# The recurrent gates' products one step behind the rounding of their tokens, and a head's squares in a buffer of their own

## The chip, the cores and the metric

The kernel runs on one core of a Trainium2 chip. Its time is the device time of one execution in microseconds (us). Three runs of the kernel before took 1630.3 to 1632.11 us, their median is 1631.26 us. Beside them stands one profiled execution of 1630.65 us.

The engines are named as the profile does: PE is TensorE (the matrix products), PEld its weight loads, DVE is VectorE, ACT is ScalarE, POOL is GpSimd, SP is the engine that issues most DMAs. Each engine takes its instructions in the order in which the program issued them to it; semaphores hold an instruction back until what it reads is there and what it overwrites has been read.

## What is computed

One layer of a diffusion backbone with 256 latent tokens, 256 context tokens and 2048 channels, all in float32. A mixer joins two groups: eight HGRN2 heads (a gated linear recurrence with a 128x128 state in both directions) and eight RG-LRU blocks. A GEGLU network with a convolution follows. What the change touches, cut to its core:

```python
def rglru_dir(xc, wa, ba, wx, bx, lam, h0):          # eight blocks of 128 channels, two directions
    r = sigmoid(einsum(xb, wa) + ba)                 # "the gates": two products per direction
    i = sigmoid(einsum(xb, wx) + bx)
    log_a = -RG_C * r * softplus(-lam)
    bterm = sqrt(-expm1(2.0 * log_a)) * i * xc
    h = linear_scan(exp(log_a), bterm, h0)

def hgrn2_readout(o, g, hg_g):                       # per head of 128 channels
    o = rmsnorm(o, hg_g)                             # needs the sum of o*o over the head's channels
    return o * silu(g)

out = concatenate([hg_l, rg_l]) @ w_out              # x += gate * rmsnorm(out), then the GEGLU network
```

`xc` is a depthwise convolution of width 4 along the tokens. The product of the layer's input with `w_in` gives 56 column blocks of 128 channels: for each head `q`, `zf`, `zb`, `v` and `g`, for each recurrent block `rx` and `rg`.

## The kernel before

Channels lie on the 128 partitions and tokens along the free axis: 256 latent tokens, with 256 context tokens behind them where they are needed. Every float32 product is made of three faster ones: weights and tokens are each split into a rounded part and the rest (`wh`, `wl` and `hh`, `hl`), and a chunk of 128 input channels gives `wh*hh + wh*hl + wl*hh` (lines 266 to 268, three matmuls of 512 or 256 columns).

**The main list.** `entries` lists the weight blocks in the order of use. The mixer's part (some 195 to 760 us) is 50 entries of `w_in`, written out in `ORDER`. A block of 1 MB lands in one of three buffers. ACT rounds each half to `wh` (line 165; for the `rg` blocks DVE does, line 163), and DVE subtracts for `wl` (line 180). Four such halves are kept, and they are split two halves ahead of use.

**Steps.** An entry of 512 tokens has four steps of 12 matmuls, one of 256 tokens two steps of 24. `run()` does three things in each step: it splits weights ahead, it calls `step()`, and it issues the step's main matmuls. `step()` lets each generator in `gens` go on to its next `yield`. So what a generator issues between two yields stands, on every engine, just before the main matmuls of one step. These matmuls are what PE has to do while other engines prepare the generator's next piece. A step of the mixer has about 2.7 us of main matmuls.

**Generators.** Three kinds run side by side in the mixer:

- `rg_all` goes through the eight recurrent blocks, one after another, with `rg_chain`. A block makes its convolution on ACT and DVE, rounds the result to `xh` (line 767) and the rest to `xl` (line 768), and `gates(0)` issues six matmuls of 512 columns (lines 776 to 778) into two banks of PSUM. Then, for each direction: two sigmoids read the banks (line 786), tanh, exp and a sum on ACT (lines 788 to 790), DVE arithmetic and a square root on ACT, and two scans on DVE. The second direction's six matmuls come at the end of the first direction's last step.
- `tree` does one head: a tree of elementwise products with copies on ACT (line 918, `kc` and `qc`) and small matmuls (line 902), then the state products (941) and the output products (951). After these, ACT copies the output and squares it (956), PE sums the squares over the channels with a column of ones (960), and DVE copies the two sums to `ssq` (961). The squares lie in the first half of `qa`, the head's tile of products of query and decay (DVE writes it for the next head in line 872). `hdone` then tells `norms` that the head has its sums.
- `mod2_all` multiplies modulation weights on DVE (line 689, 180 instructions in the whole kernel).

A `g` block's generator applies silu on ACT (975), spreads the head's scale over the partitions with two small matmuls (line 589) into a PSUM bank, and multiplies on DVE (978 and 980).

**Banks.** `sbank()` hands out two banks in turn, `sd0` and `sd1`. In the mixer they serve the gates (both at once) and, in its last part, the spread of the `g` blocks. The tag `qc` has three buffers, taken in turn.

Of the kernel before, what the change touches and what calls it, by code (L numbers as in the profile page):

```python
# [9 lines left out]
F32 = mybir.dt.float32  # L10
F32R = mybir.dt.float32r
U8 = mybir.dt.uint8
AF = mybir.ActivationFunctionType
# [5 lines left out]
T = 256  # L19
# [30 lines left out]
def dit_block_kernel(  # L50
# [20 lines left out]
    pe, act, dve, pool = nc.tensor, nc.scalar, nc.vector, nc.gpsimd  # L71
# [22 lines left out]
    def sbank(which=None):  # L94

        if which is None:
            which = turn["s"] = 1 - turn["s"]
        return pss.tile([128, 512], F32, name="sd", tag=f"sd{which}")
# [7 lines left out]
    def P(name, k=0, n=1):  # L106
        o = _SM[name] + k
        return sm[:, o:o + n]
# [312 lines left out]
    for i, (name, b) in enumerate(ORDER):  # L421
        add_s1(win[i], h1, 512 if name in ("rx", "zf", "zb", "v") else 256,
               lambda ps, name=name, b=b: afters[name](b, ps), hi="dve" if name == "rg" else "act")
# [95 lines left out]
    sp4, sp8 = P("c", 0, 16), P("c", 16, 16)  # L519
# [214 lines left out]
    hq = hp2_cm.__enter__()  # L734
# [4 lines left out]
    def wg_fetch(b):  # L739
        if b < NH:  # L740
            wgs[b] = hq.tile([128, 4, 128], F32, name="wg", tag="wg")
            nc.sync.dma_start(wgs[b], wgate[b])
# [3 lines left out]
    def rg_all():  # L746
        for b in range(NH):
            while b not in rgsrc:
                yield
            yield from rg_chain(b, rgsrc[b].rearrange("p (a t) -> p a t", a=2))  # L750
            ydone.add(b)

    def rg_chain(b, x):
        xh, xl, wh, wl = (hq.tile([128, 512], F32R, name=n, tag=n) for n in ("xh", "xl", "gh", "gl"))
        wg = wgs[b].rearrange("p a n -> p (a n)")
        act.activation(wh, wg, AF.Copy)
        dve.tensor_tensor(wl, wg, wh.bitcast(F32), op=OP.subtract)
        wg_fetch(b + 1)
        xc = hq.tile([128, 2, T], F32, name="xc", tag="xc")
        act.activation(xc, x, AF.Identity, scale=P("cw", 16 + b), bias=P("cb", b))  # L760
        for j, o, i in ((0, slice(2, T), slice(0, T - 2)), (1, slice(1, T), slice(0, T - 1)),
                        (3, slice(0, T - 1), slice(1, T))):
            dve.scalar_tensor_tensor(xc[:, :, o], x[:, :, i], P("cw", 8 * j + b), xc[:, :, o], op0=OP.mult, op1=OP.add)
            if j == 0:
                yield
        xf = xc.rearrange("p a t -> p (a t)")
        dve.tensor_copy(xh, xf)
        dve.tensor_tensor(xl, xf, xh.bitcast(F32), op=OP.subtract)
        yield

        def gates(d):
            pg = {}
            for w in (1, 0):
                pg[w] = sbank()
                c = slice((2 * d + w) * 128, (2 * d + w + 1) * 128)
                pe.matmul(pg[w], wh[:, c], xh, start=True, stop=False)
                pe.matmul(pg[w], wh[:, c], xl, start=False, stop=False)
                pe.matmul(pg[w], wl[:, c], xh, start=False, stop=True)
            return pg
        pg = gates(0)  # L780
        yield
        for d in range(2):
            k = 8 * d + b
            r, iv, th, t = (hq.tile([128, 512], F32, name=n, tag=n) for n in ("r", "iv", "th", "t"))
            for w, dst, bn in ((1, iv, "bx"), (0, r, "ba")):
                act.activation(dst, pg[w], AF.Sigmoid, bias=P(bn, k))
            yield
            act.activation(th, r, AF.Tanh, scale=sp4[:, k:k + 1])
            act.activation(r, r, AF.Exp, scale=sp8[:, k:k + 1])
            act.activation(r, r, AF.Identity, bias=ones)  # L790
            dve.tensor_tensor(iv, iv, xf, op=OP.mult)
            yield

            dve.scalar_tensor_tensor(t, th, 1.0, r, op0=OP.add, op1=OP.mult)
            dve.scalar_tensor_tensor(r, t, 4.0, r, op0=OP.subtract, op1=OP.mult)
            dve.tensor_scalar(t, r, -0.5, -1.0, op0=OP.mult, op1=OP.add)
            yield
            act.activation(th, th, AF.Sqrt)
            dve.tensor_tensor(r, r, iv, op=OP.mult)
            yield  # L800
            dve.scalar_tensor_tensor(th, th, -0.5, r, op0=OP.mult, op1=OP.mult)
            if d == 0:
                dve.tensor_tensor_scan(r[:, T:], t[:, T:], th[:, T:], 0.0, op0=OP.mult, op1=OP.add)
                dve.tensor_tensor_scan(yt[:, b, :], t[:, :T], th[:, :T], r[:, 511:512], op0=OP.mult, op1=OP.add)
            else:
                dve.tensor_tensor_scan(r[:, ::-1], t[:, ::-1], th[:, ::-1], 0.0, op0=OP.mult, op1=OP.add)
            if d == 0:
                pg = gates(1)
            yield
        dve.tensor_tensor(yt[:, b, :], yt[:, b, :], r[:, :T], op=OP.add)  # L810
# [46 lines left out]
    def q_gen(h, ps):  # L857
        while h and h - 1 not in last_product:
            yield
        q = hq.tile([128, T], F32, name="q", tag="q")  # L860
        act.activation(q, ps, AF.Sigmoid)
        yield
        dve.tensor_tensor(q, q, ps, op=OP.mult)
        yield from tree(h, q)

    def tree(h, q):
        f, k, v = hd[h]["f"], hd[h]["k"], hd[h]["v"]
        qa = hq.tile([128, 2, T], F32, name="qa", tag="qa")
# [19 lines left out]
        kc, qc = {}, {}  # L888
# [63 lines left out]
        last_product.add(h)  # L952
        yield
        act.activation(ot[:, h, :], po, AF.Copy)
        sq = qa[:, 0, :]
        act.activation(sq, po, AF.Square)
        yield
        pq = lbank()
        for b in range(2):
            pe.matmul(pq[:, b:b + 1], sq[:, b * 128:(b + 1) * 128], ones, start=True, stop=True)  # L960
        dve.tensor_copy(ssq[:, 2 * h:2 * h + 2], pq[:, 0:2])
        del hd[h]
        hdone.add(h)
# [380 lines left out]
```

## Time and profile before

| what | us |
|---|---|
| median of three runs | 1631.26 |
| profiled execution | 1630.65 |
| its span, first to last instruction | 1628.9 |
| PE busy in the span | 1566.8 |
| PEld busy | 1371.2 |
| DVE busy | 1207.4 |
| ACT busy | 891.8 |

The profiled execution is 1.75 us longer than its span: this lies ahead of the first instruction and behind the last. In a table by stretch, each line gives the stretch, its length, and for PE, PEld, DVE, ACT and POOL the busy time with the number of instructions; `PEclk` is the clock that TensorE was granted, 1.00 being 2.4 GHz and 0.50 being 1.2 GHz. Busy time is a sum over stages with different limits, so the waits of a stretch say more about it than its share. An instruction's idle time before it, in brackets in a timeline, is the time in which its engine did nothing, and the name behind the arrow is what ended it. `L776` is line 776 of the kernel.

### The profile page before, as it was taken

What the parts mean: (1) busy time and instruction counts of PE and PEld (TensorE: products, weight loads), DVE (VectorE), ACT (ScalarE), POOL (GpSimd) and SP (SyncE); (2) the same over time, 40 slices, a digit from 0 to 9 for tenths busy, and PEclk for the clock granted to TensorE, in tenths of its full rate; (3) what the DMA queues carried; (4) which work ended last, traced back from release to release, by engine and by line L of the source; (5) the groups of instructions that cost most, each with busy time, mean ns of one, the idle gap of its engine ahead of it and who ended that gap; (6) DMA issues with size and microseconds to landing.
All of it is one profiled execution on the core that took longest, in us unless ns stands there. A gap on an engine that the chain in (4) does not pass through costs nothing.

```text
span 1628.9 us, 25405 instructions
## 1 busy us (share of the span) xinstructions
PE 1566.8 (96%) x9904; PEld 1371.2 (84%) x9904; DVE 1207.4 (74%) x2033; ACT 891.8 (55%) x1284; POOL 121.0 (7%) x101
## 2 busy tenths in 40 slices
PE   7999899999999999899999999999999999999997
PEld 1355687778788888799999999999999999888886
DVE  2666597889888769678658788888888877656656
ACT  2355685767674456486455644444444445455553
POOL 0511000000000000000220111111111111000000
PEclk9999999999999999999999999999999999999999
DMA  8676544455455565536862466666666555655552
GB/s 355 236 283 225 193 162 149 158 172 174 167 197 199 183 206 186 183 124 238 318 224 94 171 228 230 226 231 226 229 227 227 201 181 190 221 184 197 191 200 110
DMA packets 75584, 329.66 MB, mean 202 GB/s; under 512 B 8392, under 2 KB 8520, under 8 KB 45128
## 3 DMA queue, kind: packets, MB, share of 16 engines
q1 hardware_dynamic: 75176, 327.53, 56.9%
q8 instruction: 77, 1.26, 0.3%
q10 hardware_dynamic: 288, 0.52, 0.1%
q14 instruction: 43, 0.35, 0.1%
HBM read 325.92 MB, written 2.10 MB: 201 GB/s over the span
## 4 chain that ended last, share of the span: by engine, by line
PE 79%; DVE 11%; ACT 4%; issue 3%; DMA 2%; POOL 1%; SPq 0%; DVEq 0%; ACTq 0%; POOLq 0%
PE mb L266 12%; PE mb L267 12%; PE mb L268 12%; PE mb L458 5%; PE lv L266 5%; PE lv L267 5%; PE lv L268 5%; PE lv L458 4%; PE sd L458 4%; PE sd L317 3%; DVE wl L180 2%; PE xb L458 2%; DVE macc L689 2%; PE sd L324 1%; PE sd L323 1%
## 5 line engine op out<-in xcount | busy, mean ns | idle before, releaser
L165 ACT ACTIVATE wh<-wf 128x1024 fp32r<-128x1024 f32 x424 | 445.3, 1058 | 508.4 <-PE mb L267 166.5
L180 DVE TENSOR_TENSOR wl<-wf,wh 128x1024 fp32r<-128x1024 f32 x440 | 535.7, 1223 | 155.1 <-ACT wh L165 151.2
L266 PE MATMUL mb<-hh,wh 128*128 128x512 f32 (+1 forms) x800 | 282.9, 354 | 0.0
L268 PE MATMUL mb<-hh,wl 128*128 128x512 f32 (+1 forms) x800 | 273.4, 342 | 0.0
L267 PE MATMUL mb<-hl,wh 128*128 128x512 f32 (+1 forms) x800 | 273.2, 342 | 0.0
L266 PE MATMUL mb<-h2h,wh 128*128 128x258 f32 x672 | 190.6, 284 | 0.0
L268 PE MATMUL mb<-h2h,wl 128*128 128x258 f32 x672 | 190.2, 283 | 0.0
L267 PE MATMUL mb<-h2l,wh 128*128 128x258 f32 x672 | 190.1, 283 | 0.0
L266 PE MATMUL lv<-h2h,wh 128*128 128x258 f32 x656 | 186.0, 284 | 0.0
L268 PE MATMUL lv<-h2h,wl 128*128 128x258 f32 x656 | 185.6, 283 | 0.0
L267 PE MATMUL lv<-h2l,wh 128*128 128x258 f32 x656 | 185.5, 283 | 0.0
L268 PEld LDWEIGHTS mb<-hh,wl 128*128 128x128 f32 x800 | 152.8, 191 | 17.9
L267 PEld LDWEIGHTS mb<-hl,wh 128*128 128x128 f32 x800 | 153.7, 192 | 15.9
L266 PEld LDWEIGHTS mb<-hh,wh 128*128 128x128 f32 x800 | 153.5, 192 | 15.3
L689 DVE SCALAR_TENSOR_TENSOR macc<-wm,cs,macc 128x512 f32<-128x512 f32 x180 | 136.3, 757 | 7.3 <-DMA wm<-in_wmod_dram 6.2
L267 PEld LDWEIGHTS mb<-h2l,wh 128*128 128x128 f32 x672 | 127.4, 190 | 0.0
L268 PEld LDWEIGHTS mb<-h2h,wl 128*128 128x128 f32 x672 | 126.9, 189 | 0.0
L266 PEld LDWEIGHTS mb<-h2h,wh 128*128 128x128 f32 x672 | 126.8, 189 | 0.0
L267 PEld LDWEIGHTS lv<-h2l,wh 128*128 128x128 f32 x656 | 124.4, 190 | 0.0
L268 PEld LDWEIGHTS lv<-h2h,wl 128*128 128x128 f32 x656 | 123.9, 189 | 0.0
L266 PEld LDWEIGHTS lv<-h2h,wh 128*128 128x128 f32 x656 | 123.7, 189 | 0.0
L1040 DVE TENSOR_TENSOR al<-actt,ah 128x256 fp32r<-128x256 f32 x88 | 37.8, 431 | 86.2 <-ACT ah L1039 86.2
(344 smaller groups left out, 2861.8 us busy)
## 6 DMA issues: line engine op xcount, KB each, us to landing
wf<-in_wup_dram SPq DMA_DIRECT2D x88, 1024.0 KB, 4.9
wm<-in_wmod_dram SPq DMA_DIRECT2D x256, 256.0 KB, 5.1
wf<-in_win_dram SPq DMA_DIRECT2D x50, 1024.0 KB, 4.8
wf<-in_wdn_dram SPq DMA_DIRECT2D x44, 1024.0 KB, 4.8
wf<-in_wmod_dram SPq DMA_DIRECT2D x32, 1024.0 KB, 5.7
wf<-in_wout_dram SPq DMA_DIRECT2D x16, 1024.0 KB, 5.1
wf<-in_wearly_dram SPq DMA_DIRECT2D x12, 512.0 KB, 5.5
oy<-in_xs_dram SPq DMA_DIRECT2D x2, 1024.0 KB, 13.4
```

The costliest lines, as they stand in the source:

```text
L165: act.activation(wh, w, AF.Copy)
L180: lo.tensor_tensor(wl, fetched[j][:, h * H:(h + 1) * H], wh.bitcast(F32), op=OP.subtract)
L266: pe.matmul(ps, wh[:, w], hh, start=(i == 0), stop=False)
L267: pe.matmul(ps, wh[:, w], hl, start=False, stop=False)
L268: pe.matmul(ps, wl[:, w], hh, start=False, stop=(i == KC - 1))
L317: pe.matmul(ps, cs[:, :, 4 * q + k], get[:, k * 512:(k + 1) * 512], start=(q == 0 and k == 0), stop=(q == 3 and k == 3))
L323: pe.matmul(ps, cc, wh[:, s], start=(q == 0 and k == 0), stop=False)
L324: pe.matmul(ps, cc, wl[:, s], start=False, stop=(q == 3 and k == 3))
L458: pe.matmul(dn["ps" + str(half)][tb * 2 + n], a[:, t], w[:, s], start=(kc == 0 and first), stop=(kc == NJ - 1 and last))
L689: dve.scalar_tensor_tensor(acc, w, cc, acc, op0=OP.mult, op1=OP.add)
L1040: dve.tensor_tensor(al, actt[:, kc, :], ah.bitcast(F32), op=OP.subtract)
```

## The change

Four edits, all in generators of the mixer:

- `rg_chain` has a `yield` between the rounding of the tokens and `gates(0)`. The six matmuls are issued in the next step, behind one step's main matmuls, and everything behind them in the block comes one step later. A block has one step more.
- In each direction, the tanh moves ahead of a `yield`, into the step of the two sigmoids.
- The squares of a head go to a buffer of the tag `qc` instead of the first half of `qa`.
- The copy to `ssq` comes a step behind the matmuls whose sums it reads, and `hdone` with it.

```diff
--- before.py
+++ after.py
@@ -777,6 +777,7 @@
                 pe.matmul(pg[w], wh[:, c], xl, start=False, stop=False)
                 pe.matmul(pg[w], wl[:, c], xh, start=False, stop=True)
             return pg
+        yield
         pg = gates(0)
         yield
         for d in range(2):
@@ -784,8 +785,8 @@
             r, iv, th, t = (hq.tile([128, 512], F32, name=n, tag=n) for n in ("r", "iv", "th", "t"))
             for w, dst, bn in ((1, iv, "bx"), (0, r, "ba")):
                 act.activation(dst, pg[w], AF.Sigmoid, bias=P(bn, k))
-            yield
             act.activation(th, r, AF.Tanh, scale=sp4[:, k:k + 1])
+            yield
             act.activation(r, r, AF.Exp, scale=sp8[:, k:k + 1])
             act.activation(r, r, AF.Identity, bias=ones)
             dve.tensor_tensor(iv, iv, xf, op=OP.mult)
@@ -952,12 +953,13 @@
         last_product.add(h)
         yield
         act.activation(ot[:, h, :], po, AF.Copy)
-        sq = qa[:, 0, :]
+        sq = hq.tile([128, T], F32, name="qc", tag="qc", bufs=3)
         act.activation(sq, po, AF.Square)
         yield
         pq = lbank()
         for b in range(2):
             pe.matmul(pq[:, b:b + 1], sq[:, b * 128:(b + 1) * 128], ones, start=True, stop=True)
+        yield
         dve.tensor_copy(ssq[:, 2 * h:2 * h + 2], pq[:, 0:2])
         del hd[h]
         hdone.add(h)
```


Behind the first added line the numbers of the changed kernel are one higher than before, behind the second two: the copy to `ssq` is line 963 there, the matmul with the ones 961, silu 977.

A row below is an instruction: its line, its operation, what it writes and reads by the program's names, its shape, and a count where it repeats.

The first place is PE's queue around the first direction's gates of the last recurrent block, where the spread of the first `g` block stands too. Before, the six matmuls of the gates come directly behind the spread:

```order
L902 MATMUL lv<-qc,kc 128x128 x2
L589 MATMUL sd<-ident,rso 128x128 x2
L776 MATMUL sd<-xh,gh 128x512
L777 MATMUL sd<-xl,gh 128x512
L778 MATMUL sd<-xh,gl 128x512
L776 MATMUL sd<-xh,gh 128x512
L777 MATMUL sd<-xl,gh 128x512
L778 MATMUL sd<-xh,gl 128x512
L266 MATMUL mb<-hh,wh 128x256
```


In the changed kernel main matmuls follow the spread (here of 256 columns, the first three of 24):

```order
L903 MATMUL lv<-qc,kc 128x128 x2
L589 MATMUL sd<-ident,rso 128x128 x2
L266 MATMUL mb<-hh,wh 128x256
L267 MATMUL mb<-hl,wh 128x256
L268 MATMUL mb<-hh,wl 128x256
```


and the gates come behind these 24 and the next level of the head's tree:

```order
L903 MATMUL lv<-qc,kc 128x128 x2
L776 MATMUL sd<-xh,gh 128x512
L777 MATMUL sd<-xl,gh 128x512
L778 MATMUL sd<-xh,gl 128x512
L776 MATMUL sd<-xh,gh 128x512
L777 MATMUL sd<-xl,gh 128x512
L778 MATMUL sd<-xh,gl 128x512
L266 MATMUL mb<-hh,wh 128x256
```


The gates have moved by one step. In the blocks before, where one block follows the other directly, the steps add up against the heads: the first block's gates stand 12 main matmuls of 512 columns later than before, and the second block's first gates have moved from the step ahead of the head's state product (941) to a step behind it.

The second place is DVE's queue around the first head's copy to `ssq`. Before, the block's arithmetic (801 to 804) and the next head's start (863 to 872) stand behind it:

```order
L689 SCALAR_TENSOR_TENSOR macc<-wm,cs,macc 128x512 x2
L180 TENSOR_TENSOR wl<-wf,wh 128x1024
L961 COPY ssq<-lv 128x2
L801 SCALAR_TENSOR_TENSOR th<-th,r 128x512
L803 SCALAR_TENSOR_TENSOR r<-t,th 128x256
L804 SCALAR_TENSOR_TENSOR oy<-t,r,th 128x256
L689 SCALAR_TENSOR_TENSOR macc<-wm,cs,macc 128x512
L711 TENSOR_TENSOR gg_1159<-rq,sm 128x4
L713 TENSOR_TENSOR gg_1159<-gg_1159,sm 128x4
L863 TENSOR_TENSOR q<-q,mb 128x256
L871 TENSOR_TENSOR ks<-k 128x256
L872 TENSOR_TENSOR qa<-f,q 128x512
```


In the changed kernel other work of the block (795 to 797) and the modulation come ahead of it:

```order
L795 SCALAR_TENSOR_TENSOR t<-th,r 128x512
L796 SCALAR_TENSOR_TENSOR r<-t,r 128x512
L797 TENSOR_SCALAR t<-r 128x512
L689 SCALAR_TENSOR_TENSOR macc<-wm,cs,macc 128x512
L711 TENSOR_TENSOR gg_1159<-rq,sm 128x4
L713 TENSOR_TENSOR gg_1159<-gg_1159,sm 128x4
L963 COPY ssq<-lv 128x2
L864 TENSOR_TENSOR q<-q,mb 128x256
L872 TENSOR_TENSOR ks<-k 128x256
L873 TENSOR_TENSOR qa<-f,q 128x512
```


The copy has moved behind a step's DVE work, and the matmul that it waits for stands a step ahead on PE.

The third place is ACT's queue from the first silu on, around the sigmoids (786) of the last block's first direction, which free the two banks `sd0` and `sd1`. Before:

```order
L975 ACT_TABLE_LOAD
L975 ACTIVATE gl<-mb 128x256
L918 ACTIVATE kc<-k 128x256
L918 ACTIVATE qc<-qa 128x256
L786 ACT_TABLE_LOAD
L786 ACTIVATE iv<-sd,sm 128x512
L786 ACTIVATE r<-sd,sm 128x512
L918 ACTIVATE kc<-k 128x256
L918 ACTIVATE qc<-qa 128x256
```


In the changed kernel:

```order
L977 ACT_TABLE_LOAD
L977 ACTIVATE gl<-mb 128x256
L919 ACTIVATE kc<-k 128x256
L919 ACTIVATE qc<-qa 128x256
L919 ACTIVATE kc<-k 128x256
L919 ACTIVATE qc<-qa 128x256
L977 ACTIVATE gl<-mb 128x256
L787 ACT_TABLE_LOAD
L787 ACTIVATE iv<-sd,sm 128x512
L787 ACTIVATE r<-sd,sm 128x512
L788 ACTIVATE th<-r,sm 128x512
```


Ahead of the load of the sigmoids' table there now stand a second pair of the tree's copies (919) and the second silu, and the tanh comes directly behind the sigmoids. Counted over the whole queue, ACT has 83 table loads instead of 82. On PE, in the same place, the spread of the second `g` block stands one step behind the gates instead of two.

## Rows read from the trace of the kernel before

**Rows 1.** The page's first lines: busy time, share of the span, instructions.

```profile
span 1628.9 us, 25405 instructions
PE 1566.8 (96%) x9904; PEld 1371.2 (84%) x9904; DVE 1207.4 (74%) x2033; ACT 891.8 (55%) x1284; POOL 121.0 (7%) x101
```

**Rows 2.** Busy time in four stretches, then granted clock, DMA share, GB/s.

```profile
200.00:300.00 100.00, 94.21 (x457) 78.61 (x456) 83.74 (x147) 69.69 (x103) 0.00 (x0) 0.96 0.47 160
300.00:400.00 100.00, 95.70 (x517) 82.15 (x517) 86.60 (x153) 71.65 (x105) 0.00 (x0) 0.97 0.51 172
600.00:700.00 100.00, 91.63 (x553) 81.09 (x552) 80.96 (x148) 62.01 (x95) 0.00 (x0) 0.95 0.53 180
700.00:745.00 45.00, 45.00 (x376) 44.54 (x376) 36.98 (x61) 33.43 (x43) 0.00 (x0) 1.00 0.39 138
```

**Rows 3.** TensorE's waits from 190 to 745 us: total, times, longest.

```profile
PE sd L776 <- DVE xh L767: 16.7, 6, 4.5
PE sd L776 <- DVE oy L980: 4.1, 1, 4.1
PE lv L902 <- DVE ad L891: 2.0, 2, 1.5
PE lv L941 <- DVE qa L936: 1.8, 1, 1.8
PE xb L704 <- ACT v L850: 1.6, 1, 1.6
```

**Rows 4.** TensorE's timeline at single stalls: start, duration, in brackets idle time.

```profile
199.58 0.76 PE L776 MATMUL sd<-xh,gh 128*128 128x512 f32 x1 [4.46 <-DVE xh L767]
246.49 0.47 PE L776 MATMUL sd<-xh,gh 128*128 128x512 f32 x1 [1.51 <-DVE xh L767]
299.44 0.47 PE L776 MATMUL sd<-xh,gh 128*128 128x512 f32 x1 [1.98 <-DVE xh L767]
349.74 0.47 PE L776 MATMUL sd<-xh,gh 128*128 128x512 f32 x1 [2.09 <-DVE xh L767]
447.93 0.76 PE L776 MATMUL sd<-xh,gh 128*128 128x512 f32 x1 [3.95 <-DVE xh L767]
685.92 0.65 PE L776 MATMUL sd<-xh,gh 128*128 128x512 f32 x1 [2.75 <-DVE xh L767]
691.87 0.79 PE L776 MATMUL sd<-xh,gh 128*128 128x512 f32 x1 [4.09 <-DVE oy L980]
```

**Rows 5.** Stretches behind four stalls, one of full clock; columns as before.

```profile
199.60:204.70 5.10, 5.10 (x12) 3.75 (x13) 5.10 (x9) 3.93 (x7) 0.00 (x0) 0.50 0.84 307
300.40:303.70 3.30, 3.30 (x13) 2.86 (x12) 3.27 (x8) 2.62 (x5) 0.00 (x0) 0.50 0.38 108
448.00:453.90 5.90, 5.90 (x14) 4.36 (x15) 5.86 (x13) 0.72 (x2) 0.00 (x0) 0.50 0.84 307
692.00:696.20 4.20, 4.20 (x17) 3.91 (x18) 2.95 (x8) 2.67 (x5) 0.00 (x0) 0.50 0.08 12
205.00:210.10 5.10, 5.10 (x24) 4.19 (x23) 5.03 (x8) 3.00 (x5) 0.00 (x0) 1.00 0.24 78
```

**Rows 6.** VectorE's waits from 190 to 745 us.

```profile
DVE ssq L961 <- PE lv L960: 16.5, 4, 5.7
DVE qa L872 <- PE lv L960: 11.2, 3, 4.4
```

**Rows 7.** Timelines of VectorE and TensorE near 248 us.

```profile
247.65 0.42 DVE L936 TENSOR_TENSOR qa<-qa,tn 128x256 f32<-128x256 f32 x1
251.13 1.24 PE L941 MATMUL lv<-qa,k 128*128 128x256 f32 x5
```

**Rows 8.** Timelines of ScalarE and TensorE in the last block.

```profile
694.25 1.28 ACT L786 ACT_TABLE_LOAD   x1
695.54 0.69 ACT L786 ACTIVATE iv<-sd,sm 128x512 f32<-128x512 f32 x1
701.20 0.61 PE L589 MATMUL sd<-ident,rso 128*128 128x128 f32 x4
```

More of the change, by code (lines that the diff above doesn't have):

```diff
@@ L786, in rg_chain @@
                 act.activation(dst, pg[w], AF.Sigmoid, bias=P(bn, k))
+            act.activation(th, r, AF.Tanh, scale=sp4[:, k:k + 1])
             yield
-            act.activation(th, r, AF.Tanh, scale=sp4[:, k:k + 1])
             act.activation(r, r, AF.Exp, scale=sp8[:, k:k + 1])
```

## The prediction

> **What bounds the kernel now.** I read the page's busy times first: PE is busy for 1566.8 of 1628.9 us [rows 1], so at most 62 us of idle time can go, and what else can go is time in which its clock is low. The table by stretch comes next, to see where that is [rows 2]. In the mixer's part PE is busy for 94 of 100 us, then 96, and for 92 between 600 and 700 us, at a mean clock of 0.95 to 0.97. From 700 to 745 us it is never idle. The change touches only this part; behind it I count nothing.
>
> The list of PE's waits says what ends its idle time there [rows 3]. The first matmul of the gates (L776) waits six times for the rounding `xh` on DVE, 16.7 us in all, and once for 4.1 us for the multiplication that still reads its bank (L980). All other waits come to 2.0 + 1.8 + 1.6 = 5.4 us. The timeline gives the seven stalls one by one: 4.46, 1.51, 1.98, 2.09, 3.95, 2.75, and 4.09 us [rows 4].
>
> A stall costs more than its idle time. In the 5.1 us behind the first one the clock is 0.50, which is 1.2 GHz, and 12 matmuls go through; from 205 us on, in as long a stretch at full clock, 24 do [rows 5]. Such a stretch therefore loses half its length. Behind the stall at 299.44 there are 3.3 us of it (and as much behind that at 349.74), behind the stall at 447.93 there are 5.9, and behind the last one 4.2. Behind that at 246.49 there is none. In every case PE had been idle just before.
>
> DVE's waits are the other half of the picture [rows 6]. It waits 16.5 us in four places for PE's sum of squares, to copy it, and 11.2 us in three places to overwrite `qa`, which that sum still reads. DVE takes its work in order, so in these 27.7 us it does nothing for PE, and a block's `xh` comes late afterwards.
>
> **The change part by part.** *The gates a step later.* No matmul is added. Between the rounding and the gates there now stand the main matmuls of one step, 12 of 512 columns. At full clock 24 such matmuls lie in 5.1 us [rows 5]; the stretch cuts one or two of them at its edges, so 12 take 2.7 us. What is left of a stall is its length less 2.7, as long as DVE's work ahead of `xh` is as late as before:
>
> - At 199.58: 4.46 - 2.7 leaves 1.8 us, so 2.7 us are gained. Its low clock costs half of 5.1, that is 2.55 us. A shorter idle time can give back all or nothing of it, and I take half, 1.3. Together 4.0 (bounds 2.7 and 5.25).
> - At 246.49: 1.51 goes. What is late next is the head's state product (L941), which now meets PE before the gates do. It starts at 251.13, and its operand is ready at 247.65 + 0.42 = 248.07 [rows 7]. Without the stall, and with the gates' six matmuls (1.4 us) behind it instead of ahead, it would start at 248.2: just in time. Gain 1.5 (bounds 0 and 1.5).
> - At 299.44: 1.98, and half of 3.3 for the clock, 1.65. Gain 3.6 (without the clock 2.0).
> - At 349.74: 2.09 and 1.65. Gain 3.75 (without the clock 2.1).
> - At 447.93: 2.7 from the step. Of the 1.25 that are left I leave half, 0.6, because DVE comes sooner (below). The low clock costs half of 5.9, 2.95. Gain 3.95 - 0.6 + 2.95 = 6.3 (bounds 2.7 and 6.9).
>
> These five come to 4.0 + 1.5 + 3.6 + 3.75 + 6.3 = 19.15 us.
>
> *The last block, 685.92 and 691.87.* Here I expect nothing. The step takes the 2.7 us away from the first stall, but the second matmul of the gates still needs the bank that L980 frees, and PE would reach it no earlier than before. The next spread (L589, at 701.20) needs a bank that the block's first sigmoid frees, at 695.54 + 0.69 = 696.23 [rows 8]: 5.0 us in hand. It will stand one step nearer to the gates, which takes 2.7 of these, and before that sigmoid ACT has to do three more activations (a pair of copies and a silu of 256 columns, each at most the 0.69 us of the sigmoid with 512: 2.1), with a wait for DVE before the copies. That uses up the 5.0 us, so what the step gives can be lost again at the next bank. I take 0, with bounds of 4 us on either side, the length of the stall at 691.87.
>
> *The squares in their own buffer, and the copy a step later.* DVE's 27.7 us of waits go: the copy finds a sum that is a step old, and the next head's `qa` waits only for the output products, which stand two steps ahead. The added buffer is one of three that are taken in turn, and the one that it takes was last read several steps before, so I count no wait. DVE's time is not PE's time; this is what makes the stalls at 299.44 and 447.93 smaller at their source, and I count it only there. The norm of the first seven heads is computed a step later; what that costs lies inside the bounds of the last block.
>
> *The tanh and the table loads.* The tanh moves, at the same cost. The queue has one more table load, 1.28 us of ACT [rows 8]. ACT is busy for about 70 of 100 us [rows 2], so I count nothing for it; on the path it would be 1.3. The Trainium skill (ScalarE: Activation LUTs, What ACT_TABLE_LOAD costs) gives 2.66 us for a switch, the load and a drain. The trace does not show the drain: the load begins at 694.25 and the sigmoid 1.29 us later, at 695.54. By the page the sum would be 1.4 us worse if the load were on the path.
>
> *What PE meets when it is earlier.* The products that wait now for 5.4 us will be met earlier still, and others that had little in hand will join them. The price is between 0 (DVE keeps up) and 8, which is 1.5 times those 5.4 us, the half being for the clock. I take 3.5, nearer to the shorter end because DVE has 27.7 us more.
>
> The sum: 19.15 + 0 - 3.5 = 15.65 us. The profiled execution (a span of 1628.9 and 1.75 us around it) would go from 1630.65 to 1615.0. The median is 0.6 us above it, so I forecast 1615.6 us. With all upper bounds (5.25 + 1.5 + 3.6 + 3.75 + 6.9 + 4 = 25, and nothing met) the median is 1606; if the waits of other products shrink by 3 us as well, 1603. With all lower ones (2.7 + 0 + 2.0 + 2.1 + 2.7 - 4 - 8 = -2.5) it is 1634.
>
> **The rivals.** *The step alone works.* The stalls shrink by up to 2.7 us each, but DVE is no earlier and the clock stays low as before: 2.7 + 1.5 + 2.0 + 2.1 + 2.7 - 3.5 = 7.5 us, which gives 1623.8. For it speaks that the removed waits of DVE lie some steps ahead of the stalls, and that DVE can lose its lead to ACT in between. Against it: the idle time would mostly be gone, and the low clock came only behind idle time.
>
> *DVE is the bound, and the waits move on.* In the three stretches DVE is busy for 81 to 87 us of 100, PE's weight loads for 79 to 82 [rows 2]. If DVE's work sets the pace, PE waits for `qa`, `ad` or `wl` what it no longer waits for `xh`, and the time stays at about 1631. The Trainium skill (Perfetto Trace Analysis, Identifying the Most-Contended Engine) judges PE by its weight loads and not by its matmuls, and would by that rule name DVE in this part. Against it stands that DVE's idle 13 to 19 us per 100 contain the waits that the change removes.
>
> *Slower: the last block's banks.* The spread at 701.20 waits for the sigmoid for 4 us or more, the clock falls for another 4.2 us as it did behind 691.87 [rows 5] (2.1 lost), and the extra table load comes onto ACT's path (1.3): 7.4 us. PE has no idle time from 700 to 745 that could take this up [rows 2]. It decides only if the other blocks give as little as their lower bounds less 8, that is 9.5 - 8 = 1.5 us. Then the time is 1631.3 + 7.4 - 1.5 = 1637.2.
>
> **How the numbers follow.** The forecast's own case has a chance of 0.66, the step alone 0.14, DVE as the bound 0.14, the banks 0.06. The range is 1603 to 1628: it holds the forecast's case nearly whole and the step alone, and leaves out most of the other two. About 0.2%, 3.3 us, is what a measurement can tell from no change. Faster by more has 0.65 of the first case, 0.13 of the second and 0.05 of the third, together 0.83; within it lie 0.09 (the third case above all), slower 0.08.
>
> **What would show it.** If these steps are right, the wait of L776 for `xh` falls from 16.7 us to below 4 in the changed profile, what is left of it stands at the first block, the stretches of half clock around 300, 350 and 448 us are gone, DVE's waits for the sum of squares fall from 27.7 us to below 3, and PE is busy for 97 us or more of 100 between 300 and 500 us. The spread L589 or the gates of the last block still wait. The forecast is wrong if the stalls stand, with the same total, at the products of the heads (L903, L942, L952, before 902, 941 and 951), if half clock remains without a stall ahead of it, or if PE's waits around 690 to 705 us exceed 7 us.

## The result, and the profile after

The changed kernel takes 1613.32 us (median of four runs, 1611.12 to 1617.64); the kernel before, run beside it, takes 1631.68 (1630.3 to 1634.98). The ratio is 0.9888, with a 95% interval of 0.9862 to 0.9913: faster by 18.4 us, or 1.1%. The forecast was 1615.6 with a range of 1603 to 1628. The profiled execution after has a span of 1612.0 us, 16.9 less than before.

The page's first lines after, against [rows 1]:

```profile
span 1612.0 us, 25404 instructions
PE 1559.0 (97%) x9904; PEld 1364.4 (85%) x9904; DVE 1207.0 (75%) x2033; ACT 894.9 (56%) x1285; POOL 122.5 (8%) x101
```

VectorE's work is what it was (1207.0 us), and PE is busy for 7.8 us less with as many matmuls: more of them ran at full clock. The table by stretch, against [rows 2], with 400 to 500 us instead of 700 to 745:

```profile
200.00:300.00 100.00, 94.88 (x508) 80.73 (x506) 88.37 (x154) 76.44 (x114) 0.00 (x0) 1.00 0.50 170
300.00:400.00 100.00, 98.39 (x525) 84.08 (x524) 90.30 (x155) 72.02 (x104) 0.00 (x0) 1.00 0.56 192
400.00:500.00 100.00, 98.50 (x579) 86.11 (x578) 92.11 (x161) 73.80 (x111) 0.00 (x0) 1.00 0.55 188
600.00:700.00 100.00, 91.41 (x587) 83.16 (x586) 82.51 (x154) 60.73 (x95) 0.00 (x0) 0.97 0.52 174
```

From 200 to 300 us PE is busy for hardly longer (94.88 for 94.21) and yet goes through 51 matmuls more, 508 for 457, at a clock of 1.00 for 0.96. The count flatters: there are 48 more of 256 columns and 6 fewer of 512, and in columns the stretch holds 5.6% more. DVE is now busy for 88 to 92 of 100 us up to 500 us. TensorE's waits from 190 to 745 us (total, times, longest), against [rows 3]; the lines are one or two higher than before:

```profile
PE sd L776 <- DVE oy L982: 4.5, 1, 4.5
PE sd L776 <- DVE xh L767: 2.7, 3, 1.6
PE sd L589 <- ACT iv L787: 2.1, 1, 2.1
PE lv L942 <- DVE qa L937: 2.0, 2, 1.7
PE lv L903 <- DVE ad L892: 2.0, 1, 2.0
PE xb L704 <- ACT v L851: 1.7, 1, 1.7
PE lv L931 <- DVE ad L892: 1.2, 1, 1.2
```

The wait for `xh` has fallen from 16.7 to 2.7 us. The wait for the bank (now L982) has hardly changed (4.5 for 4.1), the spread L589 has a new one of 2.1, and the other products have 2.0 + 2.0 + 1.7 + 1.2 = 6.9 for 5.4. The stalls one by one, against [rows 4]:

```profile
202.99 0.47 PE L776 MATMUL sd<-xh,gh 128*128 128x512 f32 x1 [1.58 <-DVE xh L767]
247.99 0.67 PE L942 MATMUL lv<-qa,k 128*128 128x256 f32 x2 [1.71 <-DVE qa L937]
304.17 0.51 PE L776 MATMUL sd<-xh,gh 128*128 128x512 f32 x1 [0.78 <-DVE xh L767]
353.40 0.49 PE L776 MATMUL sd<-xh,gh 128*128 128x512 f32 x1 [0.38 <-DVE xh L767]
617.15 0.35 PE L903 MATMUL lv<-qc,kc 128*128 128x128 f32 x1 [1.98 <-DVE ad L892]
676.54 0.80 PE L776 MATMUL sd<-xh,gh 128*128 128x512 f32 x1 [4.50 <-DVE oy L982]
684.40 0.38 PE L589 MATMUL sd<-ident,rso 128*128 128x128 f32 x1 [2.12 <-ACT iv L787]
```

The fifth block's gates, before the stall at 447.93, now start at 453.06 behind 0.15 us. The clock, in three stretches after that answer to [rows 5] (the third figure from the end of a line is the granted clock):

```profile
190.00:618.00 428.00, 417.11 (x2320) 360.04 (x2319) 366.94 (x634) 295.82 (x443) 0.00 (x0) 1.00 0.54 184
618.50:621.80 3.30, 3.30 (x18) 3.30 (x17) 3.26 (x7) 0.97 (x3) 0.00 (x0) 0.50 0.83 277
676.50:679.80 3.30, 3.26 (x12) 2.99 (x13) 3.27 (x9) 0.72 (x2) 0.00 (x0) 0.50 0.00 0
```

In this execution the clock is full from 190 to 618 us; two stretches of 3.3 us at 1.2 GHz are left, each behind a stall. Before, there were two more than the prediction counted:

```profile
266.30:269.60 3.30, 3.30 (x17) 3.30 (x17) 0.00 (x0) 2.12 (x4) 0.00 (x0) 0.50 0.36 133
686.00:692.00 6.00, 1.91 (x4) 0.72 (x4) 4.95 (x10) 2.42 (x4) 0.00 (x0) 0.50 0.74 279
```

**The sum closes.** The mixer runs from the transposition that starts it to the first wait behind it, which both traces have. Before:

```profile
188.81 0.65 PE L848 MATMUL xb<-ident,oy 128*128 128x128 f32 x4 [0.69 <-ACT oy L634]
760.00 0.39 PE L268 MATMUL mb<-mh,wl 128*128 128x256 f32 x1 [0.87 <-DVE wl L180]
```

After:

```profile
192.56 0.66 PE L849 MATMUL xb<-ident,oy 128*128 128x128 f32 x4 [0.69 <-ACT oy L634]
743.76 0.39 PE L268 MATMUL mb<-mh,wl 128*128 128x256 f32 x1 [0.88 <-DVE wl L180]
```

That is 571.2 us before and 551.2 after: 20.0 us less. In these two stretches PE goes through 3173 matmuls both times, busy for 543.45 us before and 533.21 after. So 10.2 of the 20.0 us are the clock, and 9.8 are idle time. By the prediction's terms, for this pair of executions:

| term | forecast | measured | how |
|---|---|---|---|
| first block | 4.0 | 5.4 | idle 4.46 - 1.58, all of the clock's 2.55 |
| 246 | 1.5 | 1.5 | this stall is gone |
| 299 | 3.6 | 2.9 | idle 1.98 - 0.78, clock 1.65 |
| 350 | 3.75 | 3.4 | idle 2.09 - 0.38, clock 1.65 |
| 448 | 6.3 | 6.8 | idle 3.95 - 0.15, clock 2.95 |
| low clock at 266 | none | 1.7 | half of 3.3 |
| last block | 0 | 1.6 | idle 6.84 - 6.62; clock half of (1.91 + 4.2 - 3.26) |
| met elsewhere | -3.5 | -3.2 | idle 5.4 - 6.9; clock at 618, half of 3.3 |
| sum | 15.65 | 20.0 | rounded terms; the traces give 20.0 |

The span shows 16.9 of it. Up to the mixer the two programs are the same, but this execution reached it 3.75 us later than that of before; among the 14 traces of this study the start lies between 186.5 and 192.6 us, with no relation to the edits. The eight that reach it at 190.6 us or later have a stretch at half clock between 31 and 39 us, and the six that reach it by 189.7 have none there. Behind the mixer 0.6 us are gained.

### The profile page after: what moved, and what is told of

The parts are those of the page before. It is cut to its first block, busy times and chain, and to the rows that moved or that the text cites. A ratio compares the mean times of both kernels' runs of the same rounds, so it can differ in the third digit from the quotient of the medians.

```text
span 1612.0 us, 25404 instructions
## 1 busy us (share of the span) xinstructions
PE 1559.0 (97%) x9904; PEld 1364.4 (85%) x9904; DVE 1207.0 (75%) x2033; ACT 894.9 (56%) x1285; POOL 122.5 (8%) x101
## 4 chain that ended last, share of the span: by engine, by line
PE 79%; DVE 10%; ACT 5%; issue 3%; DMA 2%; POOL 1%; SPq 0%; DVEq 0%; ACTq 0%; POOLq 0%
PE mb L266 12%; PE mb L267 11%; PE mb L268 11%; PE mb L458 5%; PE lv L266 5%; PE lv L267 5%; PE lv L268 5%; PE lv L458 4%; PE sd L458 4%; PE sd L317 3%; DVE wl L180 2%; PE xb L458 2%; DVE macc L689 2%; PE sd L324 1%; PE sd L323 1%
## 5 line engine op out<-in xcount | busy, mean ns | idle before, releaser
L180 DVE TENSOR_TENSOR wl<-wf,wh 128x1024 fp32r<-128x1024 f32 x440 | 535.8, 1223 | 160.5 <-ACT wh L165 156.6
L266 PE MATMUL mb<-h2h,wh 128*128 128x258 f32 x672 | 190.6, 284 | 0.0
L268 PEld LDWEIGHTS mb<-hh,wl 128*128 128x128 f32 x800 | 151.3, 189 | 16.9
L266 PEld LDWEIGHTS mb<-hh,wh 128*128 128x128 f32 x800 | 151.8, 190 | 14.9
```

What stands on the lines that cost most here:

```text
L180: lo.tensor_tensor(wl, fetched[j][:, h * H:(h + 1) * H], wh.bitcast(F32), op=OP.subtract)
L266: pe.matmul(ps, wh[:, w], hh, start=(i == 0), stop=False)
L268: pe.matmul(ps, wl[:, w], hh, start=False, stop=(i == KC - 1))
```

## The experiments

The theory: PE's idle time at the gates and the low clock behind it are what the change takes away, and the place of the gates in PE's queue does it. The rivals: VectorE's removed waits do it; or VectorE sets the pace and only the place of the waits changes. Times are medians, ratios are to the kernel before in the same session.

**The changed kernel again**, with no edit, in one session with the gates' step alone, both edits on the squares, and the last block's banks.

> The changed kernel once more, as the yardstick of this series. All theories: about 1613 us, a ratio to the kernel before near 0.989.

1615.15 us, ratio 0.9893 (0.9879 to 0.9906). This is the yardstick for the experiments below. Its trace is a second execution of the changed kernel, and the clock falls in other places. At 618 us there is no half clock, but there are two stretches that the first execution does not have:

```profile
264.10:267.40 3.30, 3.30 (x17) 3.30 (x17) 1.20 (x2) 3.24 (x5) 0.00 (x0) 0.50 0.36 136
451.80:455.10 3.30, 3.30 (x10) 2.52 (x9) 3.20 (x7) 1.14 (x2) 0.00 (x0) 0.50 0.76 238
```

The first lies behind the wait at L704 (1.67 us, as long as in the first execution), the second behind one of 1.18 us at L931. So a few us of half clock come and go between executions of the same kernel. The mixer is 552.4 us long here, 18.8 less than before.

**The gates' step alone**, on the kernel before:

```diff
             return pg
+        yield
         pg = gates(0)
```

> Only the first edit: the gates one step behind the rounding; tanh, squares and copy as before. Theory (two causes, the step and the vector engine's waits, which add up in part): each stall on the rounding shrinks by up to 2.7 us, 2.7 + 1.5 + 2.0 + 2.1 + 2.7 = 11 us of idle time, and the stretches of half clock behind 299 and 350 us (3.3 us in all) go; 3 or so are met elsewhere: 1620 us. The vector engine's waits for the sum of squares stay near 28 us. Rival A (the step does it all): 1613. Rival B (the vector engine's waits do it all): 1628 or more.

1616.94 us, 0.9902 (0.9886 to 0.9917): 15.6 us of the 17.4. TensorE's and VectorE's waits in this kernel, 190 to 745 us:

```profile
PE sd L776 <- DVE xh L767: 4.5, 3, 1.9
DVE ssq L962 <- PE lv L961: 16.2, 4, 6.9
DVE qa L873 <- PE lv L961: 8.3, 3, 3.4
```

VectorE still waits 24.5 us for the sum of squares, and the wait for `xh` falls from 16.7 to 4.5 all the same. The place of the gates is the cause of nearly all of the gain; VectorE's waits did not have to go for it. But the step does not act alike at every block. At the first it leaves 1.65 us of 4.46, at the fourth 0.95 of 2.09, and at the third next to nothing is won:

```profile
302.38 0.50 PE L776 MATMUL sd<-xh,gh 128*128 128x512 f32 x1 [1.90 <-DVE xh L767]
```

Two things change at once in this kernel. One step stands between the rounding and the gates, and because each block is a step longer, the later blocks' gates also stand against other work of the heads: by the count of main matmuls in PE's queue two steps later at the second block, three at the third, six at the fifth. At the first block only the distance is at work. At the others the two were not tried apart.

**Both edits on the squares alone:**

```diff
-        sq = qa[:, 0, :]
+        sq = hq.tile([128, T], F32, name="qc", tag="qc", bufs=3)
...
+        yield
         dve.tensor_copy(ssq[:, 2 * h:2 * h + 2], pq[:, 0:2])
```

> Only the last two edits: the squares in a buffer of their own and the copy of their sums a step later; gates and tanh as before. Theory: the vector engine's 27.7 us of waits go and the stalls at 299 and 448 us shrink (some 2 + 2 us and their half clock, 3), the others stay: 1624 us. Rival A (the step does it all): 1631. Rival B (the vector engine's waits do it all): 1615.

1628.09 us, 0.9974 (0.9963 to 0.9986): 4.5 us. TensorE's longest wait:

```profile
PE sd L776 <- DVE xh L767: 14.7, 6, 4.4
```

Of VectorE's 27.7 us of waits for the sum 0.8 are left, and TensorE's wait for `xh` loses 2.0 of 16.7. VectorE waits for ACT instead, at `wl` (L180) most of all, 29.2 us. 15.6 and 4.5 make 20.1, and the whole change gives 17.4. That the two halves overlap is not shown: the difference of 2.7 us lies within the three intervals, each some 2 us to either side.

**Each of these two edits by itself**, in a later session. The buffer alone (the first of the two edits):

> The kernel before with the squares in their own buffer alone. VectorE's 11.2 us of waits to overwrite qa should go, and its waits for the sum (16.5 us) stay. If what the two edits on the squares give (4.5 us) comes from qa, 1627 to 1629 us; if it comes from the copy's place, 1630 to 1632 us.

1630.98 us, 0.9995 (0.9983 to 1.0006): nothing that can be told from no change. The copy alone (the second):

> The kernel before with the later copy of the sums alone. The next head's qa stands behind the same sum whether the copy does or not: if qa is the wait that counts, VectorE waits there for nearly as long as before and the time is 1630 to 1632 us; if the copy's is the one, 1627 to 1629 us.

1628.33 us, 0.9984 (0.9973 to 0.9996): 2.6 us by the ratio. The two intervals overlap, so the times by themselves do not part the two, and neither do the totals of TensorE's wait for `xh` (15.0 and 14.9 us). The stall in TensorE's timeline at 299 us and a wait of VectorE do. With the buffer alone:

```profile
299.51 0.47 PE L776 MATMUL sd<-xh,gh 128*128 128x512 f32 x1 [1.98 <-DVE xh L767]
```

```profile
DVE ssq L961 <- PE lv L960: 16.6, 4, 5.7
```

The same two with the copy alone:

```profile
299.52 0.47 PE L776 MATMUL sd<-xh,gh 128*128 128x512 f32 x1 [0.24 <-DVE xh L767]
```

```profile
DVE qa L872 <- PE lv L960: 11.2, 3, 4.4
```

The copy's wait was the one that made `xh` late there, 1.74 us of it. What the buffer alone takes from the total lies in the last block (1.17 us for 2.75 at its first gates), where the wait for the bank behind it grows from 4.1 to 4.6. The 11.2 us at `qa` cost nothing that these runs show: they stay whole in the second kernel, and removing them gives nothing measurable in the first.

**The tanh's place alone:**

```diff
-            yield
             act.activation(th, r, AF.Tanh, scale=sp4[:, k:k + 1])
+            yield
```

> Only the second edit: the tanh in the step of the sigmoids; everything else as before. Theory: the vector engine waits less for the block's activations (17.7 us before, less 8 times 0.7, so about 12), but the tensor engine's stalls stay as they are: 1629 to 1632 us. Rival (the tanh is part of the gain): 1627 or less.

1629.80 us, 1.0001 (0.9991 to 1.0012): nothing that can be told from no change, as counted.

**A second step of distance**, on the changed kernel:

```diff
         yield
+        yield
         pg = gates(0)
```

> The changed kernel with the gates two steps behind the rounding instead of one. Theory (the step is the cure, and 2.7 us of it are left over by the stalls): the 2.7 to 3.0 us that the tensor engine still waits for the rounding go, most of it at the first block, and other products are met with other amounts: 1610 to 1614 us, so little or nothing. Rival (the longer block costs by itself, a step per block): 1616 or more.

1625.55 us, 0.9965 (0.9954 to 0.9977): most of the gain is lost. TensorE's longest waits, and behind them a row of the table by stretch, the longest of its stretches at half clock:

```profile
PE lv L904 <- DVE ad L893: 9.2, 3, 3.7
PE lv L943 <- DVE qa L938: 6.0, 3, 3.4
```

```profile
676.90:690.40 13.50, 8.09 (x30) 7.01 (x31) 11.06 (x25) 1.72 (x5) 0.00 (x0) 0.50 0.43 134
```

No wait for `xh` is left, but in these two lines the heads' products wait 15.2 us for VectorE where they waited 4.0. In the mixer this trace has 8.0 us more of idle time than the second execution of the changed kernel, and, for as many matmuls, 5.1 us more of busy time at the lower clock. A block is one step longer here and the gates fall elsewhere among the heads, so this run alone does not say which of the two does it.

**The rounding a step earlier, with TensorE's queue as it is.** On the changed kernel, the convolution and the rounding come in one step instead of two, and the step saved goes ahead of the gates:

```diff
-            if j == 0:
-                yield
...
         yield
+        yield
         pg = gates(0)
```

> The changed kernel with the convolution and the rounding of a block in one step instead of two, and a second yield ahead of the gates: TensorE's queue is the changed kernel's, instruction for instruction, and only xh and xl are issued a step earlier on VectorE. If two steps of distance failed because the block grew longer and its gates fell elsewhere among the heads, the waits for xh that the changed kernel still has (1.6 + 0.8 + 0.4 us, and 0.8 for xl) go here without new ones: 1608 to 1612 us against 1615. If they failed because VectorE has no time left and every earlier rounding makes a head's product later, the waits for ad and qa grow by as much or more: 1614 to 1626 us.

1616.53 us, 0.9916 (0.9897 to 0.9934), for 0.9893 of the changed kernel: no gain. TensorE's longest wait:

```profile
PE lv L941 <- DVE qa L936: 5.7, 3, 4.5
```

All waits for `xh` are gone from the list, and at this product there are 5.7 us for 2.0. The longest, 4.50 us, is at the second block. VectorE's timeline there, in this kernel:

```profile
243.16 0.43 DVE L765 CAST xh<-xc 128x512 fp32r<-128x512 f32 x1
244.89 0.42 DVE L936 TENSOR_TENSOR qa<-qa,tn 128x256 f32<-128x256 f32 x1
```

and in the changed kernel:

```profile
247.43 0.42 DVE L937 TENSOR_TENSOR qa<-qa,tn 128x256 f32<-128x256 f32 x1
249.33 0.43 DVE L767 CAST xh<-xc 128x512 fp32r<-128x512 f32 x1
```

Early, `xh` (and `xl` behind it) stands ahead of the head's `qa`; TensorE waits 4.50 us for it instead of 1.71. Measured from each trace's start of the mixer, `qa` is done 56.1 us on instead of 55.3: what the gates no longer wait for, the head does. In this place VectorE sets the pace, and the order of its work only decides who waits. The clock has a part too: behind the 4.50 us and behind the wait at L704 this trace has 13.3 us at 0.50, where the second execution of the changed kernel has 3.3 behind that same wait.

**More work on VectorE**, on the changed kernel: 48 multiplications of 512 columns, three per direction of a block, whose results nothing reads.

```diff
             dve.tensor_tensor(iv, iv, xf, op=OP.mult)
+            for _ in range(2):
+                dve.tensor_tensor(t, xf, xf, op=OP.mult)
...
             dve.tensor_tensor(r, r, iv, op=OP.mult)
+            dve.tensor_tensor(iv, xf, xf, op=OP.mult)
```

> The changed kernel with 48 more vector instructions of 512 columns in the recurrence (three per block and direction, 0.69 us each, 33 us in all; their results are not used). Theory (the tensor engine's queue sets the pace, the vector engine has 8 to 12 us of 100 left): most of it fits into idle time, and 5 to 12 us come through: 1618 to 1625 us. Rival (the vector engine is the bound): all of it, 1640 to 1646 us.

1636.71 us, 1.0035 (1.0022 to 1.0048), that is 0.0142 or 23 us more than the changed kernel. The page shows VectorE busy for 1238.2 us, 31.2 more. So about three quarters of the work added comes through, between the two forecasts of the expectation. TensorE's queue is the same, so the trace tells how: against the second execution of the changed kernel the mixer is 23.3 us longer, 14.0 of it idle time and 9.3 the lower clock. TensorE's longest wait is again at the heads:

```profile
PE lv L906 <- DVE ad L895: 7.1, 3, 3.4
```

**The stalls filled with work**, on the kernel before: eight matmuls of 512 columns, whose result is overwritten, ahead of each block's first gates.

```diff
+                for _ in range(fill * w):
+                    pe.matmul(pg[w], h1["hh"][:, 0, :128], h1["hh"][:, 0, :], start=True, stop=True)
...
-        pg = gates(0)
+        pg = gates(0, 8)
```

> The kernel before, with 8 matmuls of 512 columns (1.8 us) ahead of each block's first gates, into the gates' own bank, overwritten by them: the tensor engine is busy in the stall instead of idle. Theory (half of the low clock is a cost of its own): the stalls keep their ends, the half clock behind them shrinks, up to 2.5 + 1.7 + 1.7 + 3.0 us saved, and 1.8 us are lost at each of the two blocks without a stall: 1626 us. Rival (the clock does not come back, or costs nothing): 1634 to 1636 us.

1633.57 us, 1.0012 (1.0001 to 1.0023). 64 matmuls, at the 5.1 us for 24 of [rows 5], are 13.6 us of work, and the time grows by 2: the rest went into time that was lost anyway. By the traces of the two kernels TensorE's idle time in the mixer is 8.4 us less and its busy time 9.8 us more, so some 4 of the 13.6 came back from the clock. TensorE at the third block:

```profile
302.71 0.61 PE L776 MATMUL sd<-hh 128*128 128x512 f32 x2
303.46 0.47 PE L778 MATMUL sd<-xh,gh 128*128 128x512 f32 x1
```

The gates (here L778) come 0.14 us behind the last filler, and the clock of this kernel, there and behind the first block's gates:

```profile
300.40:303.70 3.30, 2.77 (x14) 2.06 (x13) 3.20 (x8) 1.68 (x3) 0.00 (x0) 1.00 0.89 349
202.50:207.60 5.10, 4.44 (x10) 3.33 (x11) 5.03 (x10) 3.22 (x6) 0.00 (x0) 0.50 0.80 304
```

Where the fillers took up the stall the clock stays full; at the first block 3.56 us of idle time are left and the clock is at half as before. So the half clock at the third block hung on the stall ahead of it. The reverse does not hold: at the fifth block 2.11 us of idle time are left, at 452.60, and the clock behind them is 1.00. The expectation of a shorter time failed: what the clock gave back did not pay for the fillers.

**The last block's banks**, on the changed kernel: the spread of the `g` blocks takes its bank from the other pair, `xbank`.

```diff
-        pb = spread(rso[:, 2 * h:2 * h + 2], 2)
+        pb = spread(rso[:, 2 * h:2 * h + 2], 2, xbank)
```

> The changed kernel, with the spread of the g blocks in the bank that the modulation sums use, so that it shares none with the gates. Theory: the tensor engine's two waits in the last block (4.5 us for the multiplication that reads the spread, 2.1 us for the sigmoid) and the half clock behind them (1.7 us) go, 8 us; some of it is met again at the weights' lower halves, where the tensor engine waits 0.9 us already: 1608 us. Rival (the vector and scalar engines set the pace from there to 745 us): the wait for the lower halves grows by what is gained, 1612 to 1614.

1610.52 us, 0.9862 (0.9849 to 0.9876): 4.6 us below the changed kernel beside it, and the fastest kernel of the study. TensorE's waits:

```profile
PE lv L903 <- DVE ad L892: 4.0, 2, 2.1
PE lv L942 <- DVE qa L937: 3.9, 1, 3.9
PE xb L589 <- DVE oy L982: 1.2, 1, 1.2
```

The two waits of the last block, 4.5 + 2.1 us, are gone, and 2.0 + 1.9 + 1.2 of them are met at other products. The trace accounts for some 2 us, half of them behind the mixer; the rest of the 4.6 stays open. With the early rounding as well:

> The same with the spread of the g blocks in the other pair of banks. If both are independent, the gain of the bank (4.6 us) adds to the gain of the early rounding: 1604 to 1608 us. If the waits only change place, no better than the bank alone: 1610 us or more.

1614.41 us, 0.9898 (0.9877 to 0.9919): the two do not add.

## Why the prediction was right

**The mechanism.** The step ahead of the gates gave by itself 15.6 of 17.4 us, though not in the same parts at every block as forecast (below). The signs that the prediction named came out in this profile: `xh` 2.7 us (below 4 asked), its longest rest at the first block, no half clock around 300, 350 and 448 us, no wait for the sum of squares left on VectorE, PE busy for 98.4 and 98.5 of 100 us from 300 to 500, and the last block's gates and spread still waiting, 4.50 and 2.12. In the second execution one of these signs comes out only in part: from 451.8 to 455.1 us the clock is at half again, where before it was for 5.9 us.

**What was sized wrongly.** The mixer gave 20.0 us, not 15.65. At the first block the clock came back whole and not by half (1.25 us); at 266 us there was a low clock that the prediction had not looked for (1.7); and in the last block the idle time stayed, as forecast, but the clock was low for 3.3 us instead of 6.1 (1.4). All three are the clock; the idle time was forecast within a microsecond in every term. Some of this is luck. At the first block's gates the clock came back whole behind 1.58 and 1.92 us in the two executions of the changed kernel, but it was at half for 3.3 us behind 1.65 us with the step alone and behind 1.89 us with the last block's other bank: half was a fair price. And the low clock at 266 us is gone in one execution of the changed kernel and there in the other, at 264 us.

**What was right for another reason.** At 448 the prediction let VectorE's freed time shrink the stall. With the squares alone it stays at 3.95 us; with the step alone, and VectorE waiting as before, 0.14 is left. The step did this; the 3.8 us are more than its 2.7, and the gates stand six steps later against the heads there. At 299 the prediction named both the step, whose 2.7 us would cover the 1.98, and VectorE's freed waits. The step alone leaves 1.90, the copy alone 0.24, and the whole change 0.78. So the freed copy won this term; neither the step nor the wait at `qa` did. At 246 the head's state product was to be just in time; it waits 1.71 us, which the term for waits met elsewhere took up.

**The rivals.** The step alone with the clock as before (1623.8) is refuted by the step alone itself: 1616.94 us, and in its mixer PE is busy for 5.0 us less than before with as many matmuls. The last block's banks cost 2.12 us at the spread, but that took the place of a stall of 2.75 at the block's first gates. VectorE as the bound is refuted as the cause of the time before, by the step alone, which took no work from VectorE, left 24.5 of the 27.7 us of its waits, and gained 15.6. The Trainium skill (Perfetto Trace Analysis, Identifying the Most-Contended Engine) judges TensorE by its weight loads, beside the share of peak operations that it reaches, and would by the weight loads have named VectorE from 200 to 400 us before (83.7 and 86.6 us of 100 against 78.6 and 82.2), though not over the whole span (74% against 84%). After the change its answer fits better: from 300 to 500 us VectorE is busy for 90 and 92 of 100 us, 31 us more of work there cost 23, and at the second block an earlier `xh` only makes `qa` later. The rival describes the kernel after better than the one before.

**The table load.** It takes 1.28 us again and the sigmoid starts 1.30 behind its start, as ScalarE's timeline in the last block shows, against [rows 8]:

```profile
681.35 0.42 ACT L919 ACTIVATE kc<-k 128x256 f32<-128x256 f32 x1 [2.45 <-DVE k L923]
...
682.36 1.28 ACT L787 ACT_TABLE_LOAD   x1
683.66 0.69 ACT L787 ACTIVATE iv<-sd,sm 128x512 f32<-128x512 f32 x1
```

Here it lies on the path, because the spread waits for that sigmoid. Ahead of both ACT has the wait that the prediction named, 2.45 us for VectorE at the tree's copies. What the load alone costs there was not tried; with the other bank nothing waits for it.

## What to carry to other kernels

When the first instruction of a group waits in an engine's queue for a neighbour that runs level with it, put other ready work between the two before trying to make the neighbour faster: here that gave 15.6 us, and taking nearly all of 27.7 us of waits from the neighbour gave 4.5. Then look at each place by itself, because a longer block also moves against its neighbours: at the third block the step won 0.1 us of 2.0. Price a stall of TensorE with the half clock that may follow it (here the clock was about half of the gain in the mixer), and look for every such stretch, not only those behind the stalls that you mean to change. Stop at the distance at which the wait is gone: here a second step, and an earlier rounding, only moved the waits to other products.

## What was not expected of the hardware

The low clock does not follow every idle time of a given length. Before, 1.6 us at L704 were followed by 3.3 us at half clock at 266 us; after, the same wait of 1.67 us at 263.55 was followed by none, nor was the 1.71 us at 247.99, while 1.98 us at 617.15 were followed by 3.3. In the second execution of the changed kernel the same two waits, 1.67 us at 263.39 and 1.98 at 619.38, change places: the first is followed by 3.3 us at half clock and the second by none. So the length of the wait does not decide by itself. What does was not tried. A comparison of two single traces therefore carries a few us of half clock that can differ between executions of one kernel.
